# Attention with the values stationary and the exponentials moving, in three of four kinds of heads

## The chip, the core and the metric

The kernel runs on one core of one Trainium2 chip as one program. The metric is the time of one execution on the device, in microseconds (us). The engines are TensorE (PE, with its weight loads shown as PEld), VectorE (DVE), ScalarE (ACT), GpSimd (POOL) and SyncE (SP, which issues most DMAs).

## The reference

Two pre-norm residual layers over 256 tokens with 1024 channels, then a final RMSNorm. Each layer projects the normalised input to the queries, keys and values of four kinds of heads, four heads of each kind. It attends, joins the sixteen outputs of 64 columns, projects them back with w_out, adds them to the residual, and runs a channel mixer: a dense SwiGLU in layer 0, the top two of eight experts in layer 1.

```python
o_a = _diff_mixer(...)      # p1 - lam * p2, then an RMSNorm of each head's output
o_b = _dilated_mixer(...)   # three dilated bands, joined by their log-sum-exp
o_c = _mla_mixer(...)       # dense causal attention on low-rank queries and keys
o_d = _swa_mixer(...)       # window of 128, two KV heads for four query heads, sinks in the denominator
x = x + jnp.concatenate([o_a, o_b, o_c, o_d], axis=-1) @ w_out[l]
```

For one head the output is softmax(scores) @ v; with sinks, exp(sink - max) is added to the denominator alone.

## The kernel before

Everything is computed in float32. Matmuls with weights are three products of high and low parts in fp32r (`mm3`, `accumulate`): each weight piece of 128x1024 is read by DMA, copied to a high part by ACT (L308), and its low part is subtracted by DVE (L309), four pieces ahead of their use. Attention matmuls are plain float32; each becomes two PE instructions with a weight load each, a transpose becomes one.

The attention stage of a layer is a list of tokens written out by hand, `ORDER[l]`. Every engine runs its instructions in the order in which this list emits them; nothing reorders them. Tokens such as `lk1` (a projection's piece), `wd1` (24 matmuls of w_out) or `c0` (a transpose) are pieces of weight work. Tokens of three characters with d, l, m or s in front are attention units: the kind (d differential, l dilated, m latent, s window with sinks; in the code g = 0, 1, 2, 3), the block t of 128 query tokens (0 or 1), and the half b of the four heads (0 or 1). Each time such a token comes up, its unit, a Python generator, runs one step further, up to its next `yield`; tokens after its end do nothing. Keys are 128 for t = 0 and 256 for t = 1.

The steps of a unit of the kinds l, m and s (`attend`), before:

1. two heads' scores on PE into a PSUM bank (`b3`, three banks); DVE adds the bias and takes the maximum (`soft`, L787).
2. ACT takes the exponentials, with their sums (L793); with sinks DVE and ACT make the sink's term (L847, L848).
3. PE transposes the exponentials, 128x128 at a time (L801).
4. ACT copies them to SBUF (`pT`, L805); DVE takes the reciprocals of the sums (L857), with sinks after an addition (L856).
5. PE multiplies: the transposed exponentials are stationary, the values, 64 columns, move; the output has tokens on partitions and goes into the one bank `pob` (L811). For b = 1, DVE then multiplies all four heads by the reciprocals (L863).
6. (b = 1) PE transposes the output, two blocks of 128x128 (L818, `finish`).
7. (b = 1) ACT copies the high part (`oT_h`, L462), DVE subtracts the low part (`oT_l`, L463): `split_evac`. They are the operands that w_out's matmuls move.

The differential units (`diff`) normalise their exponentials on DVE in a step of their own (L886 to L891), ahead of the transposes, and after the values have a chain of ACT (L904, L905), DVE (L907, L452), POOL (L453) and DVE (L909, L910) in front of `finish`. The last kind of a layer is l; its tokens stand in front of the last pieces of w_out, `ws0`, `ws1`, `z0` and `z1`.

After the attention of layer 0 comes the dense SwiGLU, after that of layer 1 the experts (`moe`), which take two thirds of the time.

Of the kernel before, what the change touches and what calls it, by code (L numbers as in the profile page):

```python
# [24 lines left out]
F32 = mybir.dt.float32  # L25
# [4 lines left out]
ALU = mybir.AluOpType  # L30
# [4 lines left out]
D = 1024  # L35
# [25 lines left out]
def _chunks(w, cols):  # L61

    k = w.shape[0] // 128
    return w.reshape(k, 128, w.shape[1])[:, :, cols].transpose(1, 0, 2)
# [51 lines left out]
def _t1_units():  # L116

    units = []
    for l in range(2):
        units += [[_piece_size(t) for t in u] for u in _layer_units(l)]  # L120
        if l == 0:
            units += [[1024, 1024]] * (3 * NF0 // 2)
    return units


def _pack_t1(w_in, w_out, w_uq, w_ukv, w1, w3, w2):
    sizes = [n for u in _t1_units() for n in u]
    units = [sum(u) for u in _t1_units()]
    starts = np.cumsum([0] + [128 * u for u in units]).tolist()
    out = np.empty(starts[-1], np.float32)  # L130
    where = []
    for i, u in enumerate(_t1_units()):
        o = 0
        for n in u:
            where.append((i, o, n))
            o += n
    done = [0]

    def put(p):
        i, o, n = where[done[0]]  # L140
        assert p.size == 128 * n, (p.shape, n)
        out[starts[i]:starts[i + 1]].reshape(128, units[i])[:, o:o + n] = p.reshape(128, n)
        done[0] += 1

    r = np.arange

    def piece(l, tok):
        w = w_in[l]
        wo = w_out[l].reshape(8, 128, D).transpose(1, 0, 2)
        k, i = tok[:-1], int(tok[-1])  # L150
        if k == "cq":
            return _chunks(w, r(C_CQ, C_CQ + 512))[:, 2 * i:2 * i + 2]
        if k == "va":
            c = np.concatenate([r(C_KPE, C_KPE + 32), r(C_VA, C_VA + 256), r(C_VD, C_VD + 128)])
            return _chunks(w, c)[:, 2 * i:2 * i + 2]
        if k == "vb":
            return _chunks(w, r(C_VB, C_VB + 256))[:, 4 * i:4 * i + 4]
        if k == "up":
            q = _chunks(w_uq[l], r(384))
            return q[:, 0:2] if i == 0 else np.concatenate([q[:, 2], _chunks(w_ukv[l], r(512))[:, 0]], axis=1)  # L160
        if k in ("dq", "dk", "lq", "lk", "sk"):
            c = {"dq": C_QA, "dk": C_KA, "lq": C_QB, "lk": C_KB, "sk": C_KD}[k] + 128 * i
            return _chunks(w, r(c, c + 128))
        if k == "sq":
            c = C_QD + 64 * i
            return _chunks(w, np.concatenate([r(c, c + 64), r(c + 128, c + 192)]))
        if k == "z":
            g = KINDS.index(LAST)
            return wo[:, 2 * g:2 * g + 2, 512 * i:512 * i + 512]
        return wo[:, 2 * KINDS.index(k[1]) + i]  # L170

    for l in range(2):
        for u in _layer_units(l):
            for tok in u:
                put(piece(l, tok))
        if l == 0:
            w2c = w2[0].reshape(NF0, 128, D).transpose(1, 0, 2)
            for i in range(NF0 // 2 + 1):
                for f in (2 * i, 2 * i + 1):
                    if f < NF0:  # L180
                        put(_chunks(w1[0], r(128 * f, 128 * f + 128)))
                        put(_chunks(w3[0], r(128 * f, 128 * f + 128)))
                for f in (2 * i - 2, 2 * i - 1):
                    if f >= 0:
                        put(w2c[:, f])
    assert done[0] == len(sizes)
    return out
# [143 lines left out]
def trunk(ctx, tc, a, out, stop=None):  # L331
    nc = tc.nc
    pe, dve, act, pool = nc.tensor, nc.vector, nc.scalar, nc.gpsimd
# [127 lines left out]
    def split_evac(h, l, src):  # L461
        act.activation(h, src, AF.Copy)  # L462
        dve.tensor_sub(l, src, h.bitcast(F32))  # L463
# [86 lines left out]
    def layer(l):  # L550
        at = ExitStack()
        ap = at.enter_context(tc.tile_pool(name=f"att{l}", bufs=1, side="right", reuse_waits="tile"))
        asm = at.enter_context(tc.tile_pool(name=f"asm{l}", bufs=1, side="right", reuse_waits="tile"))
        acc, b3, pob = bankA, bankB, bankC

        ac = ap.tile([128, N_ATT], F32, name="ac")
        causal = ac[:, 0:256]
        table = ac[:, 256:3328].rearrange("p (h k) -> p h k", h=12)
        rope = ac[:, 3328:3456].rearrange("p (t k) -> p t k", t=2)
        gm = ap.tile([128, 512], F32, name="gm", tag="pT", bufs=2)  # L560
        v = {}
# [159 lines left out]
        oT_h = big.tile([128, KC, S], F32R, name="oTh", tag="oTh")  # L721
        oT_l = big.tile([128, KC, S], F32R, name="oTl", tag="oTl")
# [74 lines left out]
        def transposed(ev, kb):  # L797
            n = 2 * kb
            p = b3()
            for i in range(n):  # L800
                pe.transpose(p[:, 128 * i:128 * i + 128],  # L801
                             ev[:, i // kb, 128 * (i % kb):128 * (i % kb) + 128], ident)
            yield
            d = ap.tile([128, 512], F32, name="pT", tag="pT", bufs=2)
            act.activation(d[:, :128 * n], p[:, :128 * n], AF.Copy)  # L805
            return d[:, :128 * n].rearrange("p (i b q) -> p i b q", i=2, b=kb)

        def values(out, pT, hh, t, vals, vsl):
            for i, h in enumerate(hh):
                for kb in range(t + 1):  # L810
                    pe.matmul(out[:, 64 * h:64 * h + 64], pT[:, i, kb, :], vals[kb][:, vsl(h)],  # L811
                              start=kb == 0, stop=kb == t)

        def finish(g, t, on):

            p = b3()
            for c in range(2):
                pe.transpose(p[:, 128 * c:128 * c + 128], on[:, 128 * c:128 * c + 128], ident)  # L818
            yield
            sl = (slice(None), slice(2 * g, 2 * g + 2), slice(128 * t, 128 * t + 128))  # L820
            split_evac(oT_h[sl], oT_l[sl], p[:, :256].rearrange("p (c t) -> p c t", c=2))

        def h4(x):
            return x.rearrange("p (h d) -> p h d", h=4)

        def head(h):
            return slice(64 * h, 64 * h + 64)

        odd_even = (slice(0, 4, 2), slice(1, 4, 2))
        in_order = (slice(0, 2), slice(2, 4))  # L830
        held = {}

        def attend(g, t, b, score, vals, vsl, heads, bias, sinks=False):

            w = 128 * (t + 1)
            hs = heads[b]
            hh = range(4)[hs]
            bank = b3()
            for i, h in enumerate(hh):
                score(bank[:, i * w:(i + 1) * w], h, t, w)  # L840
            d = asm.tile([128, 4], F32, name="dn", bufs=4)
            ev, nm, exp = soft(bank, w, lambda i: bias(hh[i])[:, 256 - w:], d,
                          lambda i: neg_sink[:, l, hh[i]:hh[i] + 1] if sinks else 3e38)
            yield
            exp()
            if sinks:
                dve.tensor_tensor(d[:, 2:4], sink_v[:, l, hs], nm, op=ALU.add)  # L847
                act.activation(d[:, 2:4], d[:, 2:4], AF.Exp)  # L848
            yield
            pT = yield from transposed(ev, t + 1)  # L850
            if b == 0:
                den = asm.tile([128, 4], F32, name="den", bufs=3)
                held[g, t] = den, pob()
            den, out = held[g, t]
            if sinks:
                dve.tensor_add(d[:, 0:2], d[:, 0:2], d[:, 2:4])  # L856
            dve.reciprocal(den[:, hs], d[:, 0:2])  # L857
            yield
            values(out, pT, hh, t, vals(), vsl)
            if b == 0:  # L860
                return
            on = ap.tile([128, 256], F32, name="on", bufs=2)
            dve.tensor_mul(h4(on), h4(out[:, :256]), den[:, :, None].to_broadcast([128, 4, 64]))  # L863
            yield
            yield from finish(g, t, on)

        def diff(t, b):
            qa, ka = v["dq"], v["dk"]
# [56 lines left out]
        def unit(g, t, b):  # L925
            if g == 0:
                return diff(t, b)
            if g == 1:
                return attend(1, t, b, s_dil, lambda: v["vb"], head, odd_even, lambda h: table[:, 4 + h])
            if g == 2:  # L930
                return attend(2, t, b, s_mla, lambda: v["vm"], head, in_order, lambda h: causal)
            return attend(3, t, b, s_swa, lambda: v["vd"], lambda h: head(h // 2), in_order,
                          lambda h: table[:, 8 + h], sinks=True)

        alive = {}
# [527 lines left out]
    with tc.manual_schedule():  # L1463
        layer(0)
# [14 lines left out]
    with tc.manual_schedule():  # L1479
        layer(1)  # L1480
# [50 lines left out]
```

## Time and profile before

| | |
|---|---|
| median of 3 runs | 1432.07 us (1430.11 to 1432.19) |
| profiled execution | 1432.1 us, its span 1430.1 us |
| granted TensorE clock, mean | 0.995 |
| layer 0, projections and attention | to about 132 us |
| dense SwiGLU | about 132 to 324 us |
| layer 1, projections and attention | about 324 to 447 us |
| experts | about 447 to 1430 us |

The span is the time from the first to the last instruction of the profiled execution. An engine's busy time is the union of its instructions. In a timeline, instructions of one engine that follow on each other with the same line and tiles are merged into one row with a count; the number in brackets is the engine's idle time ahead of the row, and behind it stands what ended it.

### The profile page before, as it was taken

Reading aid. Unit: us, or ns where it says so; the run is one execution under the profiler, and the core shown is the slowest. Engines: PE = TensorE matmul, PEld = TensorE weight load, DVE = VectorE, ACT = ScalarE, POOL = GpSimd, SP = SyncE. Lnnn points to the kernel's source line nnn. Section 1 sums busy time; section 2 is a strip of 40 time slices with the busy share of each in tenths; the row PEclk is TensorE's granted clock in tenths of the full one; section 3 lists DMA queues with packets and bytes.
Section 4 is the critical chain, followed back from the end, with each engine's and each line's share of the span. In section 5 each row is a group of like instructions: output and inputs, shape, how many; then the busy total and the mean of one; then the engine's idle time right before and its main releaser. Section 6 shows DMA issues by size and latency. Waiting matters only on the chain.

```text
span 1430.1 us, 20942 instructions
## 1 busy us (share of the span) xinstructions
PE 1410.7 (99%) x7842; PEld 1219.1 (85%) x7842; DVE 1196.4 (84%) x1516; ACT 1035.8 (72%) x1338; POOL 66.3 (5%) x67
## 2 busy tenths in 40 slices
PE   9999999999999999999999999999999999999997
PEld 7999999999988788888888888888888888888885
DVE  6776665557765999999999999999999999999996
ACT  6675544445764888888887888887888888888884
POOL 2001000002000200000000000000000000000100
PEclk9999999999999999999999999999999999999999
DMA  9823555456446999999999999999999999989881
GB/s 364 319 72 117 199 178 179 140 205 243 158 165 261 358 374 333 350 395 375 368 391 378 366 396 372 364 384 379 375 370 393 373 364 395 378 338 365 329 275 55
DMA packets 65485, 435.80 MB, mean 305 GB/s; under 512 B 8026, under 2 KB 8666, under 8 KB 16864
## 3 DMA queue, kind: packets, MB, share of 16 engines
q1 hardware_dynamic: 62496, 425.97, 79.2%
q0 software_dynamic: 2880, 8.42, 1.6%
q8 instruction: 63, 1.03, 0.3%
q14 instruction: 46, 0.38, 0.1%
HBM read 430.66 MB, written 5.77 MB: 305 GB/s over the span
## 4 chain that ended last, share of the span: by engine, by line
PE 94%; DMA 2%; DVE 1%; ACT 1%; issue 1%; SPq 0%; DVEq 0%; ACTq 0%
PE acc L457 14%; PE acc L459 14%; PE acc L458 14%; PE mm L457 7%; PE mm L459 7%; PE mm L458 7%; PE B L976 3%; PE B L975 3%; PE B L974 3%; PE A L525 3%; PE A L526 2%; PE A L527 2%; PE tp L1290 2%; PE A L597 2%; PE A L598 1%; PE A L599 1%
## 5 line engine op out<-in xcount | busy, mean ns | idle before, releaser
L309 DVE TENSOR_TENSOR wl<-raw,wh 128x1024 fp32r<-128x1024 f32 (+2 forms) x801 | 965.7, 1224 | 138.7 <-ACT wh L308 98.8
L308 ACT ACTIVATE wh<-raw 128x1024 fp32r<-128x1024 f32 (+2 forms) x801 | 844.4, 1057 | 265.5 <-PE acc L459 96.8
L457 PE MATMUL acc<-wh,g 128*128 128x512 f32 x896 | 356.8, 398 | 0.0
L458 PE MATMUL acc<-wl,g 128*128 128x512 f32 x896 | 349.5, 390 | 1.3 <-DVE wl L309 1.3
L459 PE MATMUL acc<-wh,g 128*128 128x512 f32 x896 | 349.5, 390 | 0.0
L459 PEld LDWEIGHTS acc<-wh,g 128*128 128x128 f32 x896 | 168.3, 188 | 36.4
L458 PEld LDWEIGHTS acc<-wl,g 128*128 128x128 f32 x896 | 168.5, 188 | 34.7 <-DVE wl L309 2.1
L457 PEld LDWEIGHTS acc<-wh,g 128*128 128x128 f32 x896 | 168.3, 188 | 32.6
L457 PE MATMUL mm<-wh,th 128*128 128x512 f32 x440 | 171.4, 389 | 0.0
L459 PE MATMUL mm<-wh,tl 128*128 128x512 f32 x440 | 171.2, 389 | 0.0
L458 PE MATMUL mm<-wl,th 128*128 128x512 f32 x440 | 171.2, 389 | 0.0
L459 PEld LDWEIGHTS mm<-wh,tl 128*128 128x128 f32 x440 | 82.6, 188 | 17.2
L458 PEld LDWEIGHTS mm<-wl,th 128*128 128x128 f32 x440 | 82.6, 188 | 17.2
L457 PEld LDWEIGHTS mm<-wh,th 128*128 128x128 f32 x440 | 82.6, 188 | 17.1
L976 PE MATMUL B<-xh,wl 128*128 128x256 f32 x336 | 95.2, 283 | 0.0
L974 PE MATMUL B<-xh,wh 128*128 128x256 f32 x336 | 95.1, 283 | 0.0
L975 PE MATMUL B<-xl,wh 128*128 128x256 f32 x336 | 95.1, 283 | 0.0
L974 PEld LDWEIGHTS B<-xh,wh 128*128 128x128 f32 x336 | 64.5, 192 | 0.0
L975 PEld LDWEIGHTS B<-xl,wh 128*128 128x128 f32 x336 | 64.5, 192 | 0.0
L976 PEld LDWEIGHTS B<-xh,wl 128*128 128x128 f32 x336 | 64.5, 192 | 0.0
L597 PE MATMUL A<-xh,wh 128*128 128x256 f32 x176 | 51.4, 292 | 0.0
L599 PE MATMUL A<-xh,wl 128*128 128x256 f32 x176 | 49.8, 283 | 0.0
(282 smaller groups left out, 1664.5 us busy)
## 6 DMA issues: line engine op xcount, KB each, us to landing
raw<-in_wmoe SPq DMA_DIRECT2D x324, 1024.0 KB, 7.2
raw<-in_wt SPq DMA_DIRECT2D x53, 1024.0 KB, 5.0
raw<-in_wmoe SPq DMA_DIRECT2D x24, 512.0 KB, 5.8
y_rows<-yy POOLq DMA_DIRECT2D x7, 512.0 KB, 8.3
ac<-in_att SPq DMA_DIRECT2D x2, 1728.0 KB, 13.4
raw<-in_wt SPq DMA_DIRECT2D x5, 512.0 KB, 3.5
raw<-in_wt SPq DMA_DIRECT2D x2, 960.0 KB, 9.7
raw<-in_wt SPq DMA_DIRECT2D x2, 928.0 KB, 8.5
```

The costliest lines, as they stand in the source:

```text
L308: nc.scalar.activation(h[:, sl], raw[:, sl], AF.Copy)
L309: nc.vector.tensor_sub(l[:, sl], raw[:, sl], h[:, sl].bitcast(F32))
L457: pe.matmul(o, lh, rh, start=start, stop=False, **kw)
L458: pe.matmul(o, lh, rl, start=False, stop=False, **kw)
L459: pe.matmul(o, ll, rh, start=False, stop=stop, **kw)
L525: pe.matmul(o, wh[wsl], h, start=s0, stop=False, skip_group_check=True)
L526: pe.matmul(o, wh[wsl], lo, start=False, stop=False, skip_group_check=True)
L597: pe.matmul(o, hv[:, k], xh[:, k], start=k == 0, stop=False)
L599: pe.matmul(o, lv[:, k], xh[:, k], start=False, stop=k == KC - 1)
L974: pe.matmul(o, hv[:, k], xh[:, k], start=k == 0, stop=False)
L975: pe.matmul(o, hv[:, k], xl[:, k], start=False, stop=False)
L976: pe.matmul(o, lv[:, k], xh[:, k], start=False, stop=k == KC - 1)
```

## The change

In `attend`, for the kinds l, m and s, the sides of the value matmul are exchanged. The values of two neighbouring heads (128 columns; for s, both KV heads) are stationary, and the transposed exponentials of one head, 128 tokens, move. The product is 128x128 in PSUM with the output's columns on partitions and the tokens as columns; of the two heads' halves the one that belongs to the head is used. Four heads fill the bank of 512 columns.

As the tokens are columns now, the reciprocals can't multiply the output by partition. So step 3 first takes the reciprocals of the sums and multiplies the exponentials by them in place, on DVE, and then transposes. Step 5 for b = 1 has no multiplication; it runs `split_evac` at once, two times on 64 partitions (128x256 before, 64x256 twice now), each with an ACT copy and a DVE subtraction. Steps 6 and 7 are gone; their tokens stay in the list and do nothing. For s, the rows of w_out are packed in another order on the host, since the two heads that share a block of 128 rows are others. Differential units stay as they are, and so does the list of tokens.

```diff
@@ -146,7 +146,7 @@
 
     def piece(l, tok):
         w = w_in[l]
-        wo = w_out[l].reshape(8, 128, D).transpose(1, 0, 2)
+        wo = w_out[l].reshape(16, 64, D)[[*range(12), 12, 14, 13, 15]].reshape(8, 128, D).transpose(1, 0, 2)
         k, i = tok[:-1], int(tok[-1])
         if k == "cq":
             return _chunks(w, r(C_CQ, C_CQ + 512))[:, 2 * i:2 * i + 2]
@@ -811,6 +811,13 @@
                     pe.matmul(out[:, 64 * h:64 * h + 64], pT[:, i, kb, :], vals[kb][:, vsl(h)],
                               start=kb == 0, stop=kb == t)
 
+        def values_T(out, pT, hh, t, vals, pair):
+
+            for i, h in enumerate(hh):
+                for kb in range(t + 1):
+                    pe.matmul(out[:, 128 * h:128 * h + 128], vals[kb][:, pair(h)], pT[:, i, kb, :],
+                              start=kb == 0, stop=kb == t)
+
         def finish(g, t, on):
 
             p = b3()
@@ -825,6 +832,9 @@
 
         def head(h):
             return slice(64 * h, 64 * h + 64)
+
+        def two(h):
+            return slice(128 * (h // 2), 128 * (h // 2) + 128)
 
         odd_even = (slice(0, 4, 2), slice(1, 4, 2))
         in_order = (slice(0, 2), slice(2, 4))
@@ -847,22 +857,26 @@
                 dve.tensor_tensor(d[:, 2:4], sink_v[:, l, hs], nm, op=ALU.add)
                 act.activation(d[:, 2:4], d[:, 2:4], AF.Exp)
             yield
+            if sinks:
+                dve.tensor_add(d[:, 0:2], d[:, 0:2], d[:, 2:4])
+            dve.reciprocal(d[:, 0:2], d[:, 0:2])
+            for i in range(2):
+                dve.tensor_scalar(ev[:, i], ev[:, i], d[:, i:i + 1], None, op0=ALU.mult)
             pT = yield from transposed(ev, t + 1)
             if b == 0:
-                den = asm.tile([128, 4], F32, name="den", bufs=3)
-                held[g, t] = den, pob()
-            den, out = held[g, t]
-            if sinks:
-                dve.tensor_add(d[:, 0:2], d[:, 0:2], d[:, 2:4])
-            dve.reciprocal(den[:, hs], d[:, 0:2])
+                held[g, t] = pob()
+            out = held[g, t]
             yield
-            values(out, pT, hh, t, vals(), vsl)
+            values_T(out, pT, hh, t, vals(), vsl)
             if b == 0:
                 return
-            on = ap.tile([128, 256], F32, name="on", bufs=2)
-            dve.tensor_mul(h4(on), h4(out[:, :256]), den[:, :, None].to_broadcast([128, 4, 64]))
-            yield
-            yield from finish(g, t, on)
+            o4 = out.rearrange("p (c j t) -> p c j t", c=2, j=2)
+            if sinks:
+                o4 = out.rearrange("p (j c t) -> p c j t", c=2, j=2)
+            for j in range(2):
+                own = slice(64 * j, 64 * j + 64)
+                sl = (own, slice(2 * g, 2 * g + 2), slice(128 * t, 128 * t + 128))
+                split_evac(oT_h[sl], oT_l[sl], o4[own, :, j])
 
         def diff(t, b):
             qa, ka = v["dq"], v["dk"]
@@ -926,10 +940,10 @@
             if g == 0:
                 return diff(t, b)
             if g == 1:
-                return attend(1, t, b, s_dil, lambda: v["vb"], head, odd_even, lambda h: table[:, 4 + h])
+                return attend(1, t, b, s_dil, lambda: v["vb"], two, odd_even, lambda h: table[:, 4 + h])
             if g == 2:
-                return attend(2, t, b, s_mla, lambda: v["vm"], head, in_order, lambda h: causal)
-            return attend(3, t, b, s_swa, lambda: v["vd"], lambda h: head(h // 2), in_order,
+                return attend(2, t, b, s_mla, lambda: v["vm"], two, in_order, lambda h: causal)
+            return attend(3, t, b, s_swa, lambda: v["vd"], lambda h: slice(0, 128), in_order,
                           lambda h: table[:, 8 + h], sinks=True)
 
         alive = {}
```

## Rows read from the trace of the kernel before

**Rows 1.** The page, part 1: busy us of each engine (share of the span) xinstructions.

```profile
PE 1410.7 (99%) x7842; PEld 1219.1 (85%) x7842; DVE 1196.4 (84%) x1516; ACT 1035.8 (72%) x1338; POOL 66.3 (5%) x67
```

**Rows 2.** Busy time by stage: stretch, its us, each engine's busy us (xinstructions), PEclk, DMA.

```profile
60.00:110.00 50.00, 49.75 (x391) 45.76 (x390) 35.38 (x124) 33.69 (x99) 2.23 (x2) 1.00 0.32 106
700.00:800.00 100.00, 100.00 (x460) 82.79 (x459) 93.62 (x90) 82.11 (x87) 3.16 (x3) 1.00 0.99 382
```

**Rows 3.** Groups by form: count | busy us, mean ns of one | idle us before them, releasers.

```profile
L818 PE MATMUL B<-cst,on 128*128 128x128 f32 x32 | 6.2, 286 | 0.6 <-DVE on L863 0.6
...
L857 DVE RECIPROCAL den<-dn 128x2 f32<-128x2 f32 x24 | 3.6, 159 | 0.4
...
L890 DVE TENSOR_SCALAR e<-e,dn 128x256 f32<-128x256 f32 x8 | 2.8, 350 | 0.1
```

**Rows 4.** Timeline, end of layer 0's attention: start us, us, engine, line, operation, count [idle].

```profile
123.09 0.44 PE L818 MATMUL B<-cst,on 128*128 128x128 f32 x2 [0.29 <-DVE on L863]
...
123.56 0.66 ACT L462 ACTIVATE oTh<-B 128x256 fp32r<-128x256 f32 x2 [3.91 <-PE B L818]
...
123.98 0.76 DVE L463 TENSOR_TENSOR oTl<-B,oTh 128x256 fp32r<-128x256 f32 x2 [0.95 <-ACT oTh L462]
```

**Rows 5.** Timeline of PE in layer 0: scores, transposes and value matmuls.

```profile
75.43 0.61 PE L919 MATMUL B<-mqk 96*128 96x128 f32 x4
75.88 0.60 PE L801 MATMUL B<-cst,e 128*128 128x128 f32 x4
...
89.96 0.56 PE L811 MATMUL C<-vm,pT 128*128 128x64 f32 x4
90.35 0.74 PE L801 MATMUL B<-cst,e 128*128 128x128 f32 x4
```

**Rows 6.** Timeline of DVE in layer 0: a differential unit's normalisation.

```profile
67.65 0.28 DVE L890 TENSOR_SCALAR e<-e,dn 128x128 f32<-128x128 f32 x1
67.97 0.35 DVE L891 SCALAR_TENSOR_TENSOR e<-e,dn 128x128 f32<-128x128 f32 x1
68.24 0.28 DVE L890 TENSOR_SCALAR e<-e,dn 128x128 f32<-128x128 f32 x1
```

**Rows 7.** Timeline of layer 0, m00 to m11.

```profile
80.03 0.39 PE L801 MATMUL B<-cst,e 128*128 128x128 f32 x2
...
82.94 0.43 DVE L910 TENSOR_TENSOR on<-on,rs_r 128x256 f32<-128x256 f32 x1 [0.90 <-POOL rs_r L453]
...
87.79 0.20 PEld L801 LDWEIGHTS B<-cst,e 128*128 128x128 f32 x2 [0.29 <-ACT e L793]
...
89.39 0.42 DVE L787 CUSTOM_DVE_ANT_0 s<-B,ac 128x256 f32<-128x256 f32 x1
```

**Rows 8.** Timeline of layer 1, m00, m10 and s10.

```profile
398.41 1.22 DVE L309 TENSOR_TENSOR wl<-raw,wh 128x1024 fp32r<-128x1024 f32 x1
...
398.70 0.39 PE L801 MATMUL B<-cst,e 128*128 128x128 f32 x2
...
401.83 0.20 PEld L801 LDWEIGHTS B<-cst,e 128*128 128x128 f32 x2 [0.29 <-ACT e L793]
...
403.43 0.42 DVE L787 CUSTOM_DVE_ANT_0 s<-B,ac 128x256 f32<-128x256 f32 x1
...
416.71 0.50 ACT L793 ACTIVATE e<-s,nm 128x256 f32<-128x256 f32 x1
...
417.51 0.55 PE L811 MATMUL C<-va,pT 128*128 128x64 f32 x4
...
417.90 0.94 PE L801 MATMUL B<-cst,e 128*128 128x128 f32 x7
```

**Rows 9.** Busy time by stage at the start of the expert stage.

```profile
447.00:453.70 6.70, 5.07 (x29) 2.55 (x28) 2.01 (x8) 2.97 (x7) 0.00 (x0) 1.00 0.96 380
453.80:460.60 6.80, 5.82 (x30) 5.75 (x30) 3.04 (x15) 3.06 (x11) 0.70 (x1) 0.50 1.01 428
```

**Rows 10.** Timeline of PE in the first of these stretches' end.

```profile
454.04 0.17 PE L1079 MATMUL B<-maskb,trib 128*128 128x16 bf16 x1 [1.97 <-DVE maskb L1073]
```

## The prediction

> **What bounds the kernel now.** I read the page first. Its first row says that TensorE (PE) is busy for 1410.7 us, 99% of the span of 1430.1 us [rows 1]; the profiled execution took 1432.1 us, the median of the three runs shown (1432.07), so the sums below start from 1432.1. Then the busy time by stage: in the stretch with the attention of layer 0 (60 to 110 us) PE is busy for 49.75 of 50 us, VectorE (DVE) for 35.38 and ScalarE (ACT) for 33.69; in the expert stage PE is busy for 100 of 100 us [rows 2]. PE is the bound on both sides of every edit, and it takes its instructions in order. So a microsecond for which PE waits inside the attention stage moves all later work by that microsecond, and a PE instruction that goes is a gain. Last I went through the timelines of PE, DVE and ACT token by token of the hand-written order. The reader is to see there which DVE instructions stand, by program order, ahead of each group of transposes, because the change puts DVE work directly in front of 24 such groups.
>
> **What goes.** The transposes of the finished outputs (L818) go for three of four kinds: 24 of 32. A pair is 0.39 us busy (6.2 us in 16 pairs) with a mean of 0.29 for one, so the second starts about 0.11 us after the first, and each takes about 0.11 us of PE; their group also has 0.6 us of idle time before it, such as the 0.29 us at 123.09 [rows 3, 4]. That is 24 x 0.11 + 0.6 = 3.2 us saved. The multiplication of the output by the reciprocals (L863) goes too; it is DVE work.
>
> **What becomes wider.** The value matmuls move 128 columns of exponentials where they moved 64 columns of values: 72 matmuls, two PE instructions each. Four instructions with 64 columns take 0.39 us until the next work starts (89.96 to 90.35); four with 128 columns, in the scores, take 0.45 us (75.43 to 75.88) [rows 5]. Both are near 0.11 us an instruction, about the pace of the weight loads in between, so the wider half is nearly free: 24 value steps x 0.06 = 1.4 us. The lower end is 0, where PE waits right behind the step anyhow. I take 1.4, as the row of the same form says. The Trainium skill prices it higher: TensorE: Matmul & The Clock Gate, section Back-to-back issue gap, gives about 60 cycles for up to 64 columns and 134 for 128; as an estimate that is 31 ns more for each of 144 instructions, 4.5 us, and the sum would be 3 us higher.
>
> **What is added: the normalisation ahead of the transposes.** In step 3 a unit now does, on DVE, a reciprocal (0.16 us) and two multiplications in place (0.28 us on 128 columns, 0.35 on 256), and PE's transposes, in the same step, wait for them. The differential heads already run this form (L890). From their rows an instruction that needs its predecessor starts about 0.04 us after its end, and one that doesn't starts 0.08 us before it [rows 3, 6]. So the block takes 0.66 us for t = 0 (0.18 + 0.28 + 0.28 - 0.08) and 0.80 for t = 1 (0.18 + 0.35 + 0.35 - 0.08); with sinks an addition ahead of it adds 0.17. With the 0.08 of overlap at its front and 0.03 us to PE, the last pair of transposes starts 0.61 or 0.75 us after the end of whatever DVE has in front. Before, these transposes waited for ACT's exponential alone. What matters is therefore what DVE has in front.
>
> *Behind a differential unit.* In layer 0, m00's transposes start at 80.03, and DVE has the last multiplication of d01's chain ahead, which waits for POOL and ends at 82.94 + 0.43 = 83.37. The second transpose moves from 80.14 to 83.98: 3.8 us. m10 comes after d11's chain and m11's score reductions, which end at 89.39 + 0.42 = 89.81 and, hanging on PE, move along by 3.8: 89.81 + 3.85 + 0.75 = 94.4, where the second pair stood at 87.79. That is 6.6 in all, 2.8 more [rows 7]. In layer 1 m00 stands behind a weight split that ends at 398.41 + 1.22 = 399.63: 1.4 us; m10 as in layer 0 (403.85 + 1.43 + 0.75 = 406.0, against 401.83): 2.8 more [rows 8]. Sum 10.8 us.
>
> *Behind another unit's evacuation.* Step 5 of the second half of a group now holds two ACT copies and two DVE subtractions on 64 partitions; before, it held one DVE multiplication, and the subtraction came two steps later. Two such pairs back to back stand in the trace: PE's transposes end at 123.53, the last subtraction at 123.98 + 0.76 = 124.74, so 1.21 us after PE [rows 4]. They are on 128 partitions with the same 256 columns; I take the same time, and half of it as the lower end, if partitions counted. In layer 0, m01's values end at 90.52 and m11's transposes had begun at 90.35, the last pair 0.22 us later, at 90.57 [rows 5]. Now the last pair can start at values' end + 1.21 + 0.75 = 1.96 us, so about 1.9 us later than before. The same pattern (values with evacuation, a token or two, transposes) stands at m11, s00 and s11 in layer 0 and m11, s00 and l10 in layer 1: between 1.7 (where an idle gap is swallowed) and 2.1 (with sinks), 11.5 us for the six. A seventh, s10 in layer 1, is worse: its exponentials ended on ACT at 417.21, and now stand behind the copies that wait for s01's values (end 418.06). Copies 0.65 us, exponentials 1.0, sink 0.2, block 0.97, so its last pair starts 2.8 us after those values, where it started at 417.90 + 0.22: 2.8 us [rows 8]. Sum 14.3 us.
>
> *Behind smaller things* (own sink exponential, own or a neighbour's reductions, a split): seven units, 0.2 to 1.35 us each, by the same walk 4.2 us. In the six units left DVE is done before PE arrives: nothing.
>
> What is queued behind each wait: PE's next scores and the 24-instruction weight blocks, and through them everything. ACT and DVE gain slack while PE waits; the weight splits run four pieces ahead. DVE and ACT have some 14 us of room in the 50 us stretch [rows 2], so their added busy time costs nothing by itself. The SP and POOL queues keep their order.
>
> Sum: 1432.1 + 10.8 + 14.3 + 4.2 - 3.2 + 1.4 = 1459.6 us; I write 1459.5. Own range: with half the evacuation price (0.6 x 7) and free widening it is 1454; with waits that add to each other a little more, 1466.
>
> **Rivals.** (1) *The clock falls.* At 453.8 us TensorE's granted clock goes from 1.00 to 0.50 (2.4 to 1.2 GHz) for 6.8 us, after PE has been idle for about 2 us and had little to do before [rows 9, 10]. The new waits are 1.7 to 3.8 us long and stand close together. If the clock falls in them, PE does a stretch like that at half pace and loses up to 3.4 us each time; one to four times gives 1462 to 1473. Against it: at the short waits of this trace (0.29 us in [rows 4]) the clock stays at 1.00, and none of 3 us stands in it. The Trainium skill has the rule behind it: TensorE: Matmul & The Clock Gate, section Why this matters for your kernels, warns against gaps without PE work between bursts since they bring back the half clock; the trace agrees at one place.
> (2) *Shorter waits.* If half of the waits is absorbed, because DVE runs ahead once PE is late, the result is about 1445 (1440 to 1452). For it: DVE is idle a quarter of the stretch. Against it: the long ones hang on PE's own results, so DVE can't run ahead of them.
> (3) *No wait.* DVE reaches every block before PE reaches the transposes; then only the 3.2 us saved and 0 to 1.4 us lost are left: 1428.9 to 1430.3. It decides once the DVE work in front ends 0.75 us before PE's arrival; six of 24 units have this, m00 in layer 0 misses it by 3.8 us.
>
> **How the numbers follow.** A difference under about 0.2% (2.9 us) can't be told from no change here. The worked sum 0.54, the clock 0.24, shorter waits 0.17, no wait 0.05, split between faster (0.02) and no difference (0.03). Slower is then 0.95. The range of 8 in 10 runs from 1445 (about half of the shorter-wait case out) to 1471 (the top of the clock case out).
>
> **What would show it.** In the profile after, the transposes of step 3 wait for DVE's multiplication: some 25 to 30 us of PE idle time in the two attention stretches, the longest (over 3 us) ahead of m00 in layer 0, and DVE subtractions ahead of the blocks at m11, s00, s11 and l10. The value matmuls keep their pace of about 0.11 us. The last block of output weights (ws1) starts some 0.7 us sooner behind l11's values than before (0.29 us of waiting and four transposes). The expert stage is as long as it was. I am wrong if PE's idle time there is under 10 us, or if the granted clock drops below 1.00 between 60 and 450 us.

## The result, and the profile after

The changed kernel takes 1486.38 us (median of 4 runs, 1485.57 to 1487.09) beside 1431.09 us for the kernel before (4 runs): a ratio of 1.039, interval 1.0376 to 1.0403, so 55.3 us slower. The predicted 1459.5 us had the sign right and half of the loss; the time lies 15 us above the range.

The page of the kernel after shows three things: the row that answers to [rows 1], the granted clock in 40 slices, and the group of the transposes of step 3.

```profile
PE 1435.7 (97%) x7818; PEld 1239.2 (83%) x7818; DVE 1211.4 (82%) x1564; ACT 1042.7 (70%) x1350; POOL 65.5 (4%) x67
...
PEclk9978999999977999999999999999999999999999
...
L801 PE MATMUL B<-cst,e 128*128 128x128 f32 x96 | 20.7, 333 | 31.8 <-DVE e L864 31.7
```

Two things are to be seen. PE has 24 instructions less (7818 beside 7842) and yet is busy for 25.0 us more (1435.7 beside 1410.7): its instructions have become longer. And it is idle for 31.7 us ahead of the transposes, because of DVE's multiplication (L864). Together these are 56.7 us, about the loss. The clock's row says where the first of the two comes from: it dips in the slices of the two attention stages and nowhere else after the start.

The chain of waits, PE's own: what it waited for, us in all, times, the longest.

```profile
PE B L801 <- DVE e L864: 31.7, 17, 3.6
```

Busy time by stage of the kernel after (columns as in [rows 2]): the two attention stages as wholes, then the stretches inside them at the lower clock.

```profile
60.00:155.00 95.00, 78.62 (x507) 71.90 (x505) 50.39 (x172) 45.87 (x128) 2.22 (x2) 0.82 0.20 69
398.00:500.00 102.00, 86.61 (x576) 78.43 (x574) 56.40 (x187) 49.96 (x140) 2.16 (x2) 0.85 0.30 107
...
82.20:89.00 6.80, 5.26 (x25) 5.25 (x26) 2.11 (x5) 0.70 (x1) 0.63 (x1) 0.50 0.56 190
95.80:109.40 13.60, 10.55 (x44) 9.18 (x45) 4.61 (x23) 4.66 (x15) 0.00 (x0) 0.50 0.00 1
112.90:119.70 6.80, 6.80 (x27) 5.96 (x27) 3.02 (x11) 2.29 (x7) 0.00 (x0) 0.50 0.00 0
130.00:136.80 6.80, 5.96 (x28) 5.97 (x29) 2.65 (x9) 1.83 (x3) 0.00 (x0) 0.50 0.03 8
430.30:447.30 17.00, 13.01 (x52) 10.96 (x52) 6.89 (x33) 7.08 (x25) 1.11 (x1) 0.50 0.57 236
450.80:457.60 6.80, 6.80 (x27) 5.96 (x28) 2.99 (x12) 2.27 (x7) 0.00 (x0) 0.50 0.00 0
467.90:474.70 6.80, 6.80 (x30) 6.25 (x31) 1.80 (x6) 2.75 (x7) 0.00 (x0) 0.50 0.00 0
sum 64.60, PE 55.19 PEld 49.52 DVE 24.08 ACT 21.58 POOL 1.74; mean PE 7.88 PEld 7.07 DVE 3.44 ACT 3.08 POOL 0.25
```

In the kernel before, the granted clock in the attention was 1.00 ([rows 2] for layer 0; from 398 to 443.5 us, in layer 1, as well); now seven stretches, 64.6 us in all, run at 0.50, which is 1.2 instead of 2.4 GHz. In three of the seven PE is busy without a break (112.9, 450.8 and 467.9): the wait ahead of them has just ended when the clock falls, and dense work then runs at half pace. The longest, from 430.3, begins 1.4 us behind a wait of 1.22 us, and ahead of the next one.

The timeline of PE in the kernel after (columns as in [rows 4]): the first long wait and what follows it, the second, value steps and transposes of layer 0's end, and the wait ahead of 430.3.

```profile
78.76 0.28 PE L597 MATMUL A<-xh,wh 128*128 128x256 f32 x1
78.88 0.28 PE L598 MATMUL A<-xl,wh 128*128 128x256 f32 x1
...
79.56 0.56 PE L811 MATMUL C<-va,pT 128*128 128x64 f32 x4
83.74 0.69 PE L801 MATMUL B<-cst,e 128*128 128x128 f32 x2 [3.63 <-DVE e L864]
...
84.66 0.41 PE L599 MATMUL A<-xh,wl 128*128 128x256 f32 x1
84.87 0.41 PE L597 MATMUL A<-xh,wh 128*128 128x256 f32 x1
...
96.39 0.90 PE L801 MATMUL B<-cst,e 128*128 128x128 f32 x3 [3.08 <-DVE e L864]
...
146.16 0.61 PE L818 MATMUL C<-pT,vb 128*128 128x128 f32 x4
146.60 0.60 PE L801 MATMUL B<-cst,e 128*128 128x128 f32 x4
...
428.88 0.52 PE L801 MATMUL B<-cst,e 128*128 128x128 f32 x2 [1.22 <-DVE e L864]
```

m00's transposes wait 3.63 us, as foretold; then the same matmuls with weights that followed on each other every 0.12 us (78.76, 78.88) follow every 0.21 us (84.66, 84.87). The wider value step takes 0.44 us for four instructions (146.16 to 146.60), about the 0.45 us taken from [rows 5].

Unit by unit, the waits stand against the prediction's walk like this (us; in brackets the prediction):

| ahead of | layer 0 | layer 1 | sum |
|---|---|---|---|
| behind differential units: m00, m10 | 3.63 (3.8), 3.08 (2.8) | 1.22 (1.4), 2.32 (2.8) | 10.3 (10.8) |
| behind an evacuation: m11, s00, s11; m11, s00, l10; s10 | 2.45, 2.48, 2.55 | 1.67, 2.49, 2.36; 3.41 | 17.4 (14.3) |
| behind smaller things | 2.14 in two | 1.92 in four | 4.1 (4.2) |

### The profile page after: what moved, and what is told of

The parts are those of the page before. It is cut to its first block, busy times and chain, and to the rows that moved or that the text cites. A ratio compares the mean times of both kernels' runs of the same rounds, so it can differ in the third digit from the quotient of the medians.

```text
span 1485.1 us, 20920 instructions
## 1 busy us (share of the span) xinstructions
PE 1435.7 (97%) x7818; PEld 1239.2 (83%) x7818; DVE 1211.4 (82%) x1564; ACT 1042.7 (70%) x1350; POOL 65.5 (4%) x67
## 4 chain that ended last, share of the span: by engine, by line
PE 88%; DVE 3%; ACT 1%; issue 1%; POOL 0%; DVEq 0%; ACTq 0%; POOLq 0%
PE acc L457 13%; PE acc L459 13%; PE acc L458 13%; PE mm L457 7%; PE mm L459 7%; PE mm L458 7%; PE B L990 3%; PE B L989 3%; PE B L988 3%; PE A L525 2%; PE A L526 2%; PE A L527 2%; PE tp L1304 2%; PE C L818 1%; PE B L801 1%; DVE wl L309 1%
## 5 line engine op out<-in xcount | busy, mean ns | idle before, releaser
L597 PE MATMUL A<-xh,wh 128*128 128x256 f32 x176 | 52.5, 298 | 0.0
L801 PE MATMUL B<-cst,e 128*128 128x128 f32 x96 | 20.7, 333 | 31.8 <-DVE e L864 31.7
## 6 DMA issues: line engine op xcount, KB each, us to landing
ac<-in_att SPq DMA_DIRECT2D x2, 1728.0 KB, 13.4
```

What stands on the lines that cost most here:

```text
L597: pe.matmul(o, hv[:, k], xh[:, k], start=k == 0, stop=False)
L801: pe.transpose(p[:, 128 * i:128 * i + 128], ev[:, i // kb, 128 * (i % kb):128 * (i % kb) + 128], ident)
```

## The experiments

Two theories went into them. The first: the normalisation, placed in the step of the transposes, makes PE wait for DVE work of other units, and in these waits the clock falls. The second: the new form of the product costs the time, by its wider moving side or by its evacuation in two halves. The kernel before has medians of 1431.87 us beside the first four runs, 1430.57 beside the next three and 1431.77 beside the last two.

**1. The waits filled (e1_filler).** PE does 49 extra matmuls, which nothing reads, ahead of the transposes of 14 units, eight of them 3.67 us in the trace, so 0.46 us each; everything else is as after. If the waits alone cost the time, it stays; if the clock has a share, that share comes back.

```
+FILL = {(0,'m00'): 8, (0,'m10'): 5, (0,'m11'): 3, ...}
...
-        def transposed(ev, kb):
+        def transposed(ev, kb, fill=0):
...
+            for _ in range(fill):
+                pe.matmul(p[:, 0:256], ident, cst, start=True, stop=True)
```

> The changed kernel with 49 matmuls more that PE does instead of waiting: two to eight float32 matmuls of 128x256 (identity and a constant, their result overwritten) stand ahead of the transposes of 14 units, each group a little shorter than the wait predicted there. Theory 1 (PE waits for the normalisation, and the granted clock falls because PE waits): PE has its own work in the waits, the clock stays at 1.00 in both attention stages, and the waits alone are left: 1455 to 1465 us, 22 to 31 us less than the changed kernel. Theory 2 (the transposed product itself is what costs: wider moving side, evacuations on 64 partitions): no gain, 1484 or more. Theory 3 (waits alone, the clock is beside the point): no gain either, 1484 to 1490.

Measured: 1463.89 us, ratio 1.0226 (1.0205 to 1.0246). Busy time by stage of this kernel, across the two attention stages:

```profile
60.00:140.00 80.00, 74.56 (x537) 66.37 (x536) 49.18 (x169) 44.23 (x126) 2.22 (x2) 1.00 0.24 82
398.00:490.00 92.00, 83.30 (x590) 72.40 (x587) 53.14 (x173) 45.97 (x126) 2.86 (x3) 0.99 0.40 147
```

The eight extra matmuls ahead of m00 in layer 0, and what is left of the waits:

```profile
79.64 3.67 PE L802 MATMUL B<-cst 128*128 128x256 f32 x16
...
PE B L804 <- DVE e L867: 11.2, 15, 1.3
```

More work on PE, and 22.5 us less time: the clock is back at 1.00 and 0.99, the latter because the stretch reaches into the experts' entry. What is left over the kernel before is 32.0 us (the prediction's own sum was 27.5). As an estimate, 49 extra matmuls of 0.46 us and the 11.2 us of waits that are left, less the 1.8 us that the prediction had as saved, make 31.9. So the lower clock costs at least 22.5 us of the 55. The shift of ws1 in layer 1 gives another value for it. Its first matmul in the kernel before, and in the kernel after:

```profile
437.53 0.36 PE L525 MATMUL A<-oTh,wh 128*128 128x256 f32 x1
```

```profile
493.93 0.36 PE L525 MATMUL A<-oTh,wh 128*128 128x256 f32 x1
```

It starts 56.4 us later, of which 31.7 are waits, and 1.8 us were saved by the prediction's terms (3.2 less 1.4), so 26.5 us are left for the clock.

**2. The normalisation a step earlier (e2_norm_early).** The five lines move ahead of the `yield`, behind the exponentials of the unit's own step 2.

```
+            dve.reciprocal(d[:, 0:2], d[:, 0:2])
+            for i in range(2):
+                dve.tensor_scalar(ev[:, i], ev[:, i], d[:, i:i + 1], None, op0=ALU.mult)
             yield
-            dve.reciprocal(d[:, 0:2], d[:, 0:2])
...
```

> The changed kernel with the normalisation one step earlier: in step 2, right behind the exponentials, ahead of the yield. All work is the same, DVE gets it earlier in its order. Theory 1: the waits behind differential units and behind evacuations go, all but s10 of layer 1 (some 3 us) and small ones; the clock stays up: 1429 to 1438 us. Theory 2: the product and the evacuations are as they were, so most of the loss stays: 1465 or more. Theory 3: waits go as in theory 1, so it can't be told from it here.

Measured: 1456.79 us, ratio 1.0175 (1.0156 to 1.0195). That is a miss: the waits don't go, they fall to 13.4 us in 7.

```profile
PE B L801 <- DVE e L863: 13.4, 7, 3.4
```

This row is of the chain of waits of this kernel. m10 waits 3.08 and 2.48 us, s10 2.32 and 3.43: a step earlier in the unit is not earlier on DVE where the list of tokens has another unit's chain or evacuation ahead of that step too. 30.6 us still run at 0.50.

**3. The subtractions a step later (e3_evac_late).** Step 5 only copies the two halves to SBUF, by ACT; ACT's and DVE's split of high and low part comes a step later.

```
             for j in range(2):
                 own = slice(64 * j, 64 * j + 64)
-                sl = (own, slice(2 * g, 2 * g + 2), slice(128 * t, 128 * t + 128))
-                split_evac(oT_h[sl], oT_l[sl], o4[own, :, j])
+                act.activation(o2[own], o4[own, :, j], AF.Copy)
+            yield
+            sl = (slice(None), slice(2 * g, 2 * g + 2), slice(128 * t, 128 * t + 128))
+            split_evac(oT_h[sl], oT_l[sl], o2)
```

> The changed kernel with the evacuation split: step 5 copies the output's halves to SBUF on ACT only, and the split into high and low part runs in step 6, so DVE has no subtraction ahead of the next unit's normalisation. Theory 1: the seven waits behind evacuations (m11, s00 in both layers, s11 in layer 0, s10 and l10 in layer 1; 15 to 17 us of PE idle time measured) go or shrink to under 1 us each, and so does their share of the half clock: 1447 to 1463 us, with m00 and m10 waiting as before. Theory 2: no gain or a loss, 1484 or more, since ACT and DVE have more to do. Theory 3: only the idle time goes, 1469 to 1473.

Measured: 1461.77 us (one run).

```profile
PE B L801 <- DVE e L864: 19.5, 13, 3.6
```

The waits fall from 31.7 to 19.5 us, and 30.7 us instead of 64.6 run at the lower clock. Of the seven units behind an evacuation, five have lost their wait (m11, s00 and s11 in layer 0, s00 and l10 in layer 1, but for 0.28 us ahead of each s00). Two have kept it, against what was expected: m11 (1.64) and s10 (3.01) in layer 1. Layer 0's m00 (3.63) and m10 (3.08) stand as they were. So most of the prediction's second class hangs on the evacuation, and the first doesn't.

**4. No normalisation (e4_no_norm).** The sums, reciprocals and multiplications are left out; product, orientation and evacuation stay as after. The outputs are therefore not divided.

```
-            if sinks:
-                dve.tensor_add(d[:, 0:2], d[:, 0:2], d[:, 2:4])
-            dve.reciprocal(d[:, 0:2], d[:, 0:2])
-            for i in range(2):
-                dve.tensor_scalar(ev[:, i], ev[:, i], d[:, i:i + 1], None, op0=ALU.mult)
```

> The changed kernel without the normalisation: the sums, reciprocals and the two multiplications by them are left out, so the outputs are not divided. The transposes wait for ACT's exponentials alone; product, widths and evacuations are those of the changed kernel. Theory 1: no waits, clock at 1.00: 1428 to 1433 us, the 3.2 us of transposes saved against 0 to 1.4 us for the wider side. Theory 2: the loss stays: 1465 or more; a part of it in the value matmuls would show here as time over 1434.

Measured: 2412.75 us, which is not to be compared: other numbers reach the router, and the DMA queue that moved 426 MB after moves 780 MB. The attention stages can be read all the same. Busy time by stage, layers 0 and 1, then two rows of the waits from 60 to 500 us, and the first matmul of ws1 in layer 1:

```profile
60.00:126.50 66.50, 64.86 (x503) 59.56 (x502) 41.38 (x131) 45.10 (x128) 2.22 (x2) 1.00 0.29 98
398.00:450.00 52.00, 48.66 (x370) 44.02 (x369) 28.33 (x77) 29.67 (x84) 1.62 (x2) 1.00 0.39 142
```

```profile
PE B L801 <- ACT e L793: 2.0, 1, 2.0
PE C L818 <- DVE oTl L463: 1.2, 2, 0.7
...
440.80 0.36 PE L525 MATMUL A<-oTh,wh 128*128 128x256 f32 x1
```

The clock is 1.00 in both, and ws1 of layer 1 starts 3.3 us later than before, where it started 56.4 us later with the normalisation. The same matmul ahead of the attention (L597, near 60 us) stands at 60.07 us before, 59.99 after and 59.70 here, so the attention itself costs 3.6 us in this run. Product, width and evacuation together cost no more than that, and the three waits shown, all behind an evacuation, are 3.2 us. As the main cost, the second theory falls.

**5. The normalisation early, and four tokens moved (e5_early_reorder).** On top of experiment 2, the step that normalises m10 stands ahead of d11's chain in both layers, and s10's ahead of the block wd0.

```
-    m01 d11 m11 m10 m10 m01 ...
+    m01 m10 d11 m11 m10 m01 ...
...
-    ... l10 s11 s10 wd0 s10 s10 s01 ...
+    ... l10 s11 s10 s10 wd0 s10 s01 ...
```

> The kernel of e2_norm_early (1456.8 us; PE still waits 13.4 us, 11.3 of them at m10 and s10 of both layers) with four tokens moved: in both layers m10's step 2 ahead of d11's step 7, so that DVE normalises m10 before d11's chain, and s10's step 2 ahead of wd0 and, in layer 1, of s01's evacuation. Theory 1 (a wait is as long as the DVE and ACT work in front by program order): s10's waits go to under 0.5 us, m10's from 2.5 to 3.1 down to 1 to 1.5 us, with 0.5 to 1.5 us of new waiting where d11's chain is later; the clock stays up in most of the stretch: 1437 to 1446 us. If the waits come from the amount of work and not from its place: 1453 to 1460, as e2.

Measured: 1452.99 us, ratio 1.0158 (1.0139 to 1.0176), a miss again. m10's waits fall from 3.1 and 2.5 to 1.1 and 1.2 us and s10's from 2.3 and 3.4 to 1.7 and 0.6, as they should, but m01 now stands behind d11's chain and waits 2.4 us in both layers. All in all the waits are 11.5 us, and 20.5 us of the attention run at the lower clock. Moving one unit past a chain handed the wait to the next unit. Experiments 2 and 3 in one kernel weren't tried.

**6. The normalisation alone (e6_norm_only).** The kernel before, with its product and its transposes of the output; only the normalisation goes to step 3, and DVE's multiplication of the output becomes a copy.

```
+            dve.reciprocal(d[:, 0:2], d[:, 0:2])
+            for i in range(2):
+                dve.tensor_scalar(ev[:, i], ev[:, i], d[:, i:i + 1], None, op0=ALU.mult)
             pT = yield from transposed(ev, t + 1)
...
-            dve.tensor_mul(h4(on), h4(out[:, :256]), den[:, :, None].to_broadcast([128, 4, 64]))
+            dve.tensor_copy(on, out[:, :256])
```

> The kernel before with one part of the change alone: the three kinds normalise their exponentials in step 3, ahead of the transposes; product (exponentials stationary, 64 columns of values moving), output transposes and evacuations stay as before, and the multiplication of the output becomes a copy. Theory 1: m00 and m10 wait as in the changed kernel (10.5 us over both layers), the units behind another's value step wait about 1.1 us each in place of 2 (one DVE copy in front, not two ACT copies and two subtractions), smaller ones as there: 18 to 24 us of PE idle time, the clock falls in the long ones: 1458 to 1478 us. Theory 2 (the transposed product and its evacuation cost): 1430 to 1436.

Measured: 1479.87 us, ratio 1.0345 (1.0327 to 1.0364), 2 us above what was expected. The chain of waits of this kernel, and busy time by stage:

```profile
PE B L801 <- DVE e L854: 21.9, 14, 3.6
```

```profile
60.00:140.00 80.00, 68.96 (x442) 62.28 (x440) 46.07 (x167) 39.12 (x115) 2.22 (x2) 0.81 0.21 69
398.00:490.00 92.00, 80.80 (x531) 73.25 (x530) 50.66 (x175) 43.14 (x122) 2.16 (x2) 0.83 0.29 105
```

The place of the normalisation alone gives 49 of the 55 us: 21.9 us of waits, and some 61 us at the lower clock; the new product with its evacuation adds the other 6.5. With less waiting than after (21.9 beside 31.7), the clock is down almost as long. It takes no long wait for that: one of the stretches begins at 126.7, in a wait of 1.17 us, 2 us behind one of 0.94.

```profile
127.06 1.11 PE L801 MATMUL B<-cst,e 128*128 128x128 f32 x4 [1.17 <-DVE e L854]
...
126.70:130.10 3.40, 3.04 (x14) 3.04 (x15) 2.26 (x6) 0.60 (x1) 0.00 (x0) 0.51 0.32 133
```

**7. The new product where DVE is done in time (e7_hybrid_l).** The kernel before, but kind l, the last of a layer, has the transposed product, normalised in step 2. The other kinds are untouched.

```
+            if g == 1:
+                dve.reciprocal(d[:, 0:2], d[:, 0:2])
+                for i in range(2):
+                    dve.tensor_scalar(ev[:, i], ev[:, i], d[:, i:i + 1], None, op0=ALU.mult)
+                yield
...
+                values_T(out, pT, hh, t, vals(), two)
```

> The kernel before with the transposed product for the dilated heads (l) alone, their normalisation in step 2 as in e2_norm_early; m and s stay as before. Eight output transposes go and the 0.29 us wait at each layer's end; eight value steps are wider. The l units have weight blocks between their steps. Theory 1: DVE is done before PE arrives, no wait over 0.3 us, clock at 1.00: 1429.0 to 1431.5 us, 0 to 2 us less than before. Theory 2: a third of the units carry a third of the loss: 1440 or more.

Measured: 1429.69 us (11 runs) beside 1430.57 (15 runs), ratio 0.9992 (0.9983 to 1.0001): no difference that can be told, on the faster side. Busy time by stage in the two attention stages:

```profile
60.00:126.50 66.50, 66.19 (x523) 61.29 (x522) 45.80 (x158) 43.72 (x124) 2.22 (x2) 1.00 0.28 96
398.00:443.50 45.50, 45.25 (x352) 41.63 (x352) 29.37 (x99) 27.72 (x80) 1.11 (x1) 1.00 0.45 163
```

PE has no new wait above 0.2 us. ws1 starts 1.5 us sooner in layer 0 and 2.3 us in layer 1, but 0.9 us of this is there ahead of the attention already (59.16 beside 60.07 us for the matmul named in experiment 4), so the change itself gives 0.6 and 1.4 us. The third rival, no wait, comes true for kind l here, where the normalisation stands a step earlier than in the change and the other kinds are as before; in the changed kernel l11, l00 and l10 wait 1.2 to 2.4 us. Which of the two differences does it, no run separates.

**8. Both copies first (e8_copies_first).** In the evacuation of after, both of ACT's copies are issued ahead of both of DVE's subtractions, to see why the evacuation takes longer than it was priced.

```
+            for j, sl in enumerate(sls):
+                act.activation(oT_h[sl], o4[sl[0], :, j], AF.Copy)
+            for j, sl in enumerate(sls):
+                dve.tensor_sub(oT_l[sl], o4[sl[0], :, j], oT_h[sl].bitcast(F32))
```

> The changed kernel with the four evacuation instructions of step 5 in another order: both ACT copies are issued first, then both DVE subtractions. In the changed kernel's trace the second copy waits for the first subtraction, so an evacuation ends 1.73 us after PE, where the prediction had 1.21. If that order is what the evacuation term was short of, the seven units behind an evacuation wait about 0.5 us less each: PE's idle time at the transposes falls from 31.7 to 27.5 to 29 us, and the time with its share of the half clock to 1478 to 1483 us. If the second copy waits for something else, nothing changes: 1485 to 1488.

Measured: 1484.82 us, ratio 1.0371 (1.0354 to 1.0388), not as expected: 1.6 us under after, and the two intervals overlap. First the timeline of the evacuation of m01 in the kernel after, then the same in this one:

```profile
100.36 1.06 PE L818 MATMUL C<-pT,vm 128*128 128x128 f32 x4
...
101.45 0.38 ACT L462 ACTIVATE oTh<-C 64x256 fp32r<-64x256 f32 x1 [1.26 <-PE C L818]
101.86 0.42 DVE L463 TENSOR_TENSOR oTl<-C,oTh 64x256 fp32r<-64x256 f32 x1 [1.25 <-ACT oTh L462]
102.31 0.38 ACT L462 ACTIVATE oTh<-C 64x256 fp32r<-64x256 f32 x1 [0.48 <-DVE oTl L463]
102.72 0.43 DVE L463 TENSOR_TENSOR oTl<-C,oTh 64x256 fp32r<-64x256 f32 x1 [0.45 <-ACT oTh L462]
103.16 0.17 DVE L862 RECIPROCAL dn<-dn 128x2 f32<-128x2 f32 x1
103.36 0.61 DVE L864 TENSOR_SCALAR e<-e,dn 128x256 f32<-128x256 f32 x2
...
103.86 1.09 PE L801 MATMUL B<-cst,e 128*128 128x128 f32 x4 [2.45 <-DVE e L864]
```

```profile
102.18 0.77 ACT L878 ACTIVATE oTh<-C 64x256 fp32r<-64x256 f32 x2 [1.26 <-PE C L818]
...
102.98 0.86 DVE L880 TENSOR_TENSOR oTl<-C,oTh 64x256 fp32r<-64x256 f32 x2 [1.64 <-ACT oTh L878]
103.85 0.17 DVE L862 RECIPROCAL dn<-dn 128x2 f32<-128x2 f32 x1
```

After: copy, subtraction, copy, subtraction, each waiting for the one before it, though the second copy reads and writes other partitions than the first subtraction. PE's values end at 101.42 and the last subtraction at 103.15, 1.73 us later, where 1.21 had been taken from [rows 4]. With both copies first, the subtractions wait for the second copy, and the whole takes as long (values' end at 102.14, last subtraction's at 103.84: 1.70 us). Why the two engines take turns here, and didn't in [rows 4], stays open; the two halves stand in the same tiles and the same PSUM bank, which no run here separates.

**9. Only the longest waits filled (e9_filler_four).** Experiment 1 with extra matmuls, which nothing reads, ahead of m00 in layer 0, of m10 in both and of s10 in layer 1 only.

```
-FILL = {(0,'m00'): 8, (0,'m10'): 5, (0,'m11'): 3, ...}
+FILL = {(0,'m00'): 8, (0,'m10'): 5, (1,'m10'): 5, (1,'s10'): 5}
```

> As e1_filler, but with the additional matmuls ahead of four units only, those with the longest waits: m00 of layer 0, m10 of both layers, s10 of layer 1 (2.3 to 3.6 us in the changed kernel); the waits of 1.2 to 2.5 us stay empty. If the long waits alone bring the clock down, it stays at 1.00 and the time is that of e1: 1461 to 1466 us. If waits of some 2.5 us that stand close together do so too (m11 and s00 in both layers, s11 and l11 in layer 0, s11 and l10 in layer 1), the clock still falls there, less often: 1468 to 1480 us.

Measured: 1477.12 us, ratio 1.0313 (1.0292 to 1.0333). The chain of waits and busy time by stage of this kernel:

```profile
PE B L804 <- DVE e L867: 22.1, 15, 2.6
```

```profile
60.00:140.00 80.00, 70.53 (x467) 63.70 (x465) 45.95 (x160) 39.58 (x115) 2.23 (x2) 0.89 0.19 67
398.00:490.00 92.00, 80.44 (x560) 72.79 (x559) 53.80 (x177) 45.93 (x129) 2.16 (x2) 0.93 0.30 107
```

No wait is over 2.6 us, and still the clock's mean is 0.89 and 0.93, with 30.6 us at 0.50, in six stretches. The kernel is 13.2 us slower than that of experiment 1. So it isn't only the few waits of over 3 us that bring the clock down. Five of the stretches begin in or just behind a wait of 2.4 to 2.6 us, the sixth (426.5) 1.4 us behind one of 1.22 us. On the other side, the wait of 2.36 us ahead of l10 in layer 1 brings no fall, here and after, and neither do the 15 waits of at most 1.3 us in experiment 1. The length of one wait doesn't decide it; what does, these runs don't show.

## Why the prediction failed

**The bound, and that the loss begins with the waits: right.** Every edit that fills or shortens the waits (1, 2, 3, 5) gives time back; without the normalisation the attention costs 3.6 us (4).

**The waits: right within 2.4 us**, 31.7 beside 29.3. *Behind a differential unit* was 0.5 us too much. *Behind another unit's evacuation* was 3.1 us too little: its price of 1.21 us was taken from two pairs that overlap, and these don't, 1.73 us (8). That partitions don't count was taken rightly: ACT's copy takes 0.38 us on 64 partitions and on 128 (8). *Behind smaller things* was 0.1 us off.

**What goes and what becomes wider: right.** ws1 starts 0.9 us sooner in both layers, counted from the start of the last row of value matmuls (1.7 us behind it in place of 2.6), where 0.7 was forecast, and a value step takes 0.44 us, where 0.45 was; in this row of sixteen the wider ones take no longer (1.71 us beside 1.73), so the 1.4 us are an upper end. The estimate from the Trainium skill (TensorE: Matmul & The Clock Gate, section Back-to-back issue gap), 31 ns more for each instruction, doesn't hold here: four instructions went from 0.39 to 0.44 us, 13 ns more for each. The section gives the two figures for a matmul by itself, and says that in a stream of weight loads and matmuls both set the pace.

**The likeliest case: wrong.** The step that failed is the clock. "The worked sum" was given 0.54 on the premise that PE does all else at its old pace; the clock's fall got 0.24, against it the short waits of 0.29 us, none of which is near the new ones. The only row on a wait of the size forecast, 1.97 us with the clock at 0.50 around it [rows 9, 10], spoke for it. The prediction set it apart because PE "had little to do before", and that is misread: in the kernel before, PE is busy without a break up to that wait.

```profile
447.00:452.05 5.05, 5.05 (x29) 2.50 (x28) 0.55 (x2) 1.35 (x3) 0.00 (x0) 1.00 0.96 370
```

The new waits have the same effect, though PE was busy for 99% of the 50 us around them before. A clock under 1.00 between 60 and 450 us was also what the prediction named as a sign that it is wrong. That gaps without PE work between bursts bring back the half clock is also what the Trainium skill says (TensorE: Matmul & The Clock Gate, section Why this matters for your kernels); the trace agrees in seven stretches, and most of them stand at gaps shorter than the one that the page names.

**The rival's size: too small.** "Up to 3.4 us each time; one to four times" makes 13.6 us at most. The runs show 64.6 us at half clock, nine and a half times the 6.8 us of [rows 9], and 22.5 to 26.5 us lost (1), so 2.4 to 2.8 us for each 6.8. The count was wrong, not the price. The prediction gives no working for "one to four times"; four of its waits were of 2.8 us or more. The runs show that waits of 2.4 to 2.6 us count too (9), and at times shorter ones (6, 9), and two of the stretches run on over the next waits for 13.6 and 17 us.

**The sum again with the measured terms.** 1432.1 + 31.7 (waits) - 1.8 (saved less widened) + 26.5 (clock) = 1488.5; the entry into the experts, which was at half clock for 6.8 us before and is so for 3.4 us now, gives 1.4 back: 1487.1, the profiled execution's time. This closes by construction, since the clock's term is itself the rest at ws1 of layer 1 and the 1.4 is the rest behind it; experiment 1 measures the clock by other means, 22.5.

**The other rivals.** *Shorter waits*: no; DVE is idle for nearly half of the stretch (50.39 us busy of 95), yet waits don't shrink; the evacuations in front hang on PE's results (8). *No wait*: seen for kind l alone, normalised a step earlier and with the other kinds as before (7).

## What to carry to other kernels

Work that moves from behind a product to in front of it is priced by what already stands in its engine's queue at the new place, not by its own length: 0.75 us of normalisation cost PE up to 3.6 us, and moving it a step or a token only handed the wait on. Where TensorE, busy all the time, gets new waits of 1 to 3.6 us close together, add the clock's fall as a term of the sum, not as a rival: here 31.7 us of waits brought another 22.5 to 26.5 us. And a form that saves little, such as 3.2 us in 1432, can only pay at the places where the row in front shows room; at the one kind tried alone here it cost nothing, and gave nothing that can be told in the time.

## What the runs showed of the hardware

- TensorE's clock fell from 1.00 to 0.50 in a stage in which PE was still busy for 83% of the time (78.62 of 95 us), and three times it did so only as the wait ended, for 6.8 us in which PE had no break. One fall came 1.4 us behind a wait of 1.22 us, while 15 waits of up to 1.3 us (experiment 1) and one of 2.36 us went by without one.
- Extra matmuls that nothing reads made the kernel 22.5 us faster, by keeping the clock up (1486.4 to 1463.9 us).
- ACT's copy and DVE's subtraction of the two partition halves of one tile took turns, 1.73 us in place of 1.21; with both copies issued first it was 1.70 us.
- ACT and DVE take as long for 64 partitions as for 128: medians of 378 and 422 ns on 64x256, beside 383 and 424 ns on 128x256 in the trace after.
